# A decoder layer on one TensorE: the pooling mixer's value projection as two Strassen units inside the gates' pass

## The chip, the cores and the metric

The kernel runs on one core of a Trainium2 chip. The metric is the device time of one execution in microseconds. The table further down gives three runs and one profiled execution.

## The reference, cut to what matters

One layer is computed on 1040 rows: 16 learned meta tokens, then 1024 tokens of width 1024. All data are float32. The part that the change touches:

```python
u = rmsnorm(h, mix_norm_pre[l])
proj = u @ w_in[l]
q, f_logit, i_in, g_out, v_pool, gate_a, gate_b = jnp.split(proj, cuts, axis=-1)
a = hgrn2(q, f_logit, i_in, g_out, lbs[l], hgrn_out_norm[l])
p = multiscale_pool(v_pool, pool_proj[l], pool_scale[l])
z = (sigmoid(gate_a) * (a @ w_branch_hgrn[l]) + sigmoid(gate_b) * (p @ w_branch_pool[l]))
```

`q`, `f_logit`, `i_in`, `g_out` and `v_pool` are 512 wide, the two gates 1024. `hgrn2` is a gated recurrence over four heads of 128, evaluated in chunks; the gate `g_out` multiplies its output at the end. `multiscale_pool` takes for each of four groups of 128 channels the mean over the last 2, 4, 8 or 16 rows less the row itself, and then a 128x128 matrix for each group. After `z` come `w_out`, a norm, a gated feed-forward part with a causal convolution (width 2816) and another norm.

## The kernel before, in words

Every float32 product is made of three matmuls: each operand is split into a rounded high part and the rest, and high times high, high times low and low times high are added in PSUM. Features lie in partitions and rows (time) in the free dimension. `uhi` and `ulo` hold the normed input as eight blocks of 128 features by 1040 rows. SBUF work space is a pool of 24 equal slots of 1040 floats (`slot`, line 89); a tile that is taken when all are in use waits for a release. Weights go through rings of three buffers each (`wraw`, `whi`, `wlo`).

The stages in order:

1. The value pass (up to line 1057) norms the input, transposes it and computes `i_in` for the heads. While it ends, sums of quarters of the input are begun (`gate_steps`, line 966), for Strassen. `SUMS_AT` (line 39) says after which step which part of these sums is put in the queues.
2. Two early output gates (`EARLY_G` = 2), G0 and G1, are plain projections (`proj`, line 175: 8 feature blocks, 3 chunks of rows, 3 passes, 72 matmuls). Their sigmoids go to DRAM (`gscr`, line 777) and are read back when their head needs them (line 752).
3. The gates' pass (lines 997 to 1083). Class `Strassen` (line 191) computes 256 columns at a time, a unit, with seven products in place of eight, of half the features and about half the rows each. P1, P2, P6 and P4 stream 514 columns (two halo rows more), P3, P5 and P7 512. A product of 514 is cut in two (line 276). Eight units make both gates. The first `EARLY` = 4 units, in pairs, have P1 and P2 computed ahead (`start_pair`, line 322), because these two need no sums; the result of P1 is kept in a slot. The other products come in `rest` (line 328). `load_unit` (line 240) loads a unit's weights and has POOL add four sums of them; `ahead` (line 211) splits the operands of the next four products, on ACT and DVE (for some of the early ones on POOL, line 230). `put_gate` (line 838) adds up the results on DVE, takes the sigmoid on ACT and stores to DRAM.
4. The head pass (lines 1103 to 1133), in the order written in `ORDER` (line 45): F, Q, G and PV are projections of 72 matmuls, `c` is the chain of gate arithmetic with cumulative sums (`chain_f`, line 592), `h` the next of eight steps of a head (`head_steps`, line 612), PP the 128x128 matrix of a pooling group, `sp` the mean and split ahead of it (`pool_split`, line 808), `sa` the split of a head's output, BB and BA the branch products, and `w` the splitting of weights for the feed-forward part. PV (`post_pv`, line 792) copies the projection to `vp` and has POOL make the trailing sums by doubling. `eng` and `POOLED` (line 48) say which elementwise steps go to POOL instead of DVE. In a head's steps 2 to 4 matmuls make decayed scores for six levels, which masked copies put into `sc` (`level_out`, line 657: eight copies of 64 columns, one for each chunk; line 725: one of 128 columns for each chunk). Step 6 builds the chunk states (`ds`, `st`), step 7 the output (`po`), step 8 norms it (`ms`).
5. `w_out`, the feed-forward part and the last norm, which also use Strassen.

In the value pass and in the early part of the gates' pass the order on ACT, DVE and PE is the program's (line 1002). Elsewhere a planner orders the instructions of each engine by its own costs and by the order in which they are written. Each engine's queue is strictly in order; nearly all transfers are issued on SP's queue, also in order. Transfers that add into DRAM, in the feed-forward part, are issued on POOL (lines 1308, 1309, 1326).

Of the kernel before, what the change touches and what calls it, by code (L numbers as in the profile page):

```python
# [14 lines left out]
P = 128  # L15
D = 1024
SEQ = 1024
NM = 16
# [29 lines left out]
POOLED = ("e1k.0 e1k.3 kdmul.2 kdmul.3 kdsub.2 lk32.1 lk4.1 lk64.0 lq16.1 lq16.3 lq32.0 lq32.1 lq32.2 lq4.0 "  # L48
          "lq64.0 lq64.3 lq8.0 lq8.1 lq8.2 osg.2 qsmul.2 qsmul.3 sub2.2 sub32.1 sub4.1 sub8.1 sub8.3 wBA2 wBA6 "
          "wBA7 wBB2 wF0 wF2 wF3 wPP2 wPV0 wPV1 wPV2 wPV3 wQ0 wQ1 wQ3").split()  # L50
# [7 lines left out]
def trunk_kernel(ctx: ExitStack, tc: tile.TileContext, x, meta_tokens, mix_norm_pre,  # L58
# [10 lines left out]
    sm = ctx.enter_context(tc.tile_pool(name="sm", bufs=4))  # L69
# [19 lines left out]
    def slot(n, dtype=F32, name="s"):  # L89
        return stage["fm", "p"].tile([P, n], dtype, tag="fm", name=nm(name), padded_shape=[P, L])  # L90

    def ubig(dtype, name, n=KD * L):
        return upool.tile([P, n], dtype, tag="u", name=nm(name), padded_shape=[P, KD * L])
# [19 lines left out]

    open_pool("fm", FM_SLOTS)
    open_pool("ps", 8, PSUM)
# [75 lines left out]
    class Strassen:  # L191
# [8 lines left out]
        def __init__(self, units, run, early, quarters, halo, put, whole):  # L200
            self.units, self.run, self.early, self.bq = units, run, early, quarters
            self.halo, self.put, self.whole = halo, put, whole
# [65 lines left out]
        def product(self, u, p, onto=None):  # L268
# [19 lines left out]
            self.ahead(self.lead)  # L288
            return x if onto is not None else (x if self.whole_pair else x[:, o0 : o0 + n])
# [3 lines left out]
        def span(self, u, p="P1"):  # L293
# [3 lines left out]
            return (0, 512 - HN // 2 - HALO, HT) if self.halo(u) else (HALO, 0, HN)  # L297

        def own(self, u, t):
            return t[:, HALO:] if self.halo(u) else t  # L300

        def half(self, key, i, n, name):

            if key not in self.halves:
                self.halves[key] = slot(2 * HT, name=name)
            return self.halves[key][:, i * HT : i * HT + n]
# [107 lines left out]
    uhi = uhi_f.rearrange("p (k t) -> p k t", k=KD)  # L414
    ulo = ulo_f.rearrange("p (k t) -> p k t", k=KD)
# [148 lines left out]

    def V(c, h):
# [7 lines left out]

# [18 lines left out]
    def chain_f(h, kk, b, f, f2):  # L592
# [8 lines left out]
        for t0, rows in row_tiles:  # L601
            dve.tensor_tensor_scan(b[:, t0 : t0 + rows], f[:, t0 : t0 + rows], f[:, t0 : t0 + rows],
                                   0.0, ALU.add, ALU.bypass)
# [8 lines left out]
    def head_steps(h):  # L612
# [44 lines left out]
        def level_out(lv, ps, pm):  # L657
            if lv >= 32:
# [5 lines left out]
                return  # L664
            o4 = sc.rearrange("p (c b two h) -> p c b two h", c=NCH, two=2, h=lv)[:, :, :, 1, :]
            p4 = ps.rearrange("p (c b h) -> p c b h", c=NCH, h=lv)
            m3 = masks[lv].rearrange("p (b h) -> p b h", h=lv)
            for c in range(NCH):
                dve.copy_predicated(o4[:, c], m3, p4[:, c])
# [48 lines left out]
        for j in range(2):  # L718
# [4 lines left out]
            for i in range(4):  # L723
                c = 4 * j + i
                dve.copy_predicated(sc[:, c * P : (c + 1) * P], mbase, ps[:, i * P : (i + 1) * P])
# [24 lines left out]
        if h < EARLY_G:  # L750
            sgs[h] = slot(TQ, name="sg")
            nc.sync.dma_start(sgs[h], sgd[h])
# [20 lines left out]
        sg = sgs[h]  # L773
        eng(f"osg.{h}").tensor_tensor(o, o, sg, ALU.mult)
        heads[h] = dict(o=o)

    sgd = dram.tile([EARLY_G, P, TQ], F32, name="gscr")

    def post_g(h, pg):
        sg = slot(TQ, name="sg")  # L780
        for (lo, n), ps in zip(CH_Q, pg):
            act.activation(sg[:, lo : lo + n], ps[:, :n], AF.Sigmoid)
        if h < EARLY_G:
            nc.sync.dma_start(sgd[h], sg)
        else:
            sgs[h] = sg


    pooled, pin = {}, {}
    phi, plo = [None] * HEADS, [None] * HEADS  # L790

    def post_pv(g, pv):
        w = POOL_WINDOWS[g]
        vp, s1 = slot(L, name="vp"), slot(L, name="s1")
        s2 = slot(L, name="s2") if w > 2 else None
        for (lo, n), ps in zip(CH_ALL, pv):
            act.copy(vp[:, lo : lo + n], ps[:, :n])
# [8 lines left out]
        pooled[g] = (cur, vp)  # L806

    def pool_split(g):
        w = POOL_WINDOWS[g]
        cur, vp = pooled[g]  # L810
# [6 lines left out]
        pin[g] = split(cur[:, T0:L], "pl")  # L817
# [18 lines left out]
    sd = dram.tile([2 * KD, P, TQ], F32, name="sscr")  # L836

    def put_gate(u, i, h, a, b, c=None):
        at = slice(HT, TQ) if h else slice(0, HT)
# [5 lines left out]
        nc.sync.dma_start(sd[2 * u + i, :, at], g)  # L845

# [18 lines left out]
    def job(kind, i):  # L865
# [6 lines left out]
        if kind == "PV":  # L872
            return (wblock(WIN, 0, KD, CV + i * P, P), KD, u_all, CH_ALL, lambda r: post_pv(i, r))
# [72 lines left out]
    for q, i, t0, n in (("b11", 0, T0, HT), ("b21", 1, T0, HT), ("b22", 1, T0 + HT, HN)):  # L946
# [3 lines left out]
    def two_halves(dst, q):  # L950
        n = HN if q in ("t1", "t3") else HT
# [3 lines left out]
    def halo_sums(bq, d):  # L955
# [4 lines left out]
        t4 = small([P, 4 * HALO], "t4", "t4", 2).rearrange("p (k t) -> p k t", k=4)  # L960
# [5 lines left out]
    def gate_steps(d):  # L966
# [4 lines left out]
        s_ = slice(d.start - HALO, d.stop - HALO)  # L971
        a, b = (slice(T0 + d.start + o, T0 + d.stop + o) for o in (0, 512))
# [4 lines left out]
        else:  # L977
# [18 lines left out]
    ds = [slice(0, HALO)] + [slice(HALO + i * P, HALO + (i + 1) * P) for i in range(4)]  # L996
    gates = Strassen([(WIN, c + 2 * P * j) for c in (CA, CB) for j in range(KD // 2)], range(KD), EARLY, gq,
                     lambda u: True, put_gate, lambda u, i: None)
# [3 lines left out]
    with tc.manual_schedule(engines={E.Activation, E.DVE, E.PE}):  # L1002
# [34 lines left out]
        for i in range(2, len(vtiles)):  # L1037
# [11 lines left out]
            if i == 5:  # L1049
                for q in ("t2", "t1", "t3", "t4"):  # L1050
                    two_halves(gq, q)
                sums = [gate_steps(d) for d in ds]
            if i == len(vtiles) - 1:
                gl = Loader([job("G", h)[:2] + (P,) for h in range(EARLY_G)])
# [3 lines left out]
        gates.load_first(0)  # L1058
        gates.load_first(1)
        gates.ahead(2)  # L1060
        for h in range(EARLY_G):
            src, n_k, xs, chunks, post = job("G", h)
            r = proj(None, 0, n_k, xs, chunks, ws=gl.next(), name="pg")
            for j in SUMS_AT.get(9 + 2 * h, ()):
                next(sums[j], None)
            post(r)
            if h == 0:
                dve.tensor_tensor(vmeta[:NM], vm_hl[:NM], vm_low[:NM], ALU.add)
                gates.load_first(2)
                gates.ahead(4)  # L1070
            for j in SUMS_AT.get(10 + 2 * h, ()):
                next(sums[j], None)
# [3 lines left out]
        gates.load_first(3)  # L1076
# [603 lines left out]
```

## Time and profile before

| what | us |
|---|---|
| median of three runs | 1365.33 |
| lowest and highest of them | 1363.51, 1367.08 |
| the profiled execution | 1363.17 |
| its span, first to last instruction | 1361.5 |
| PE busy | 1336.0 |
| DVE busy | 952.4 |

PE is TensorE's matmuls, PEld its weight loads, DVE VectorE, ACT ScalarE, POOL GpSimd, SP SyncE. Matmuls overlap: one has a duration, but the next may start before it ends, so what matmuls cost is read from the distance of their starts. A group's row has its line, engine, operation, tiles and shapes, count, busy time, mean duration of one in ns, and the idle time of the engine before them with what ended it. A row "A <- B" tells that engine and tile A waited for B.

### The profile page before, as it was taken

Reading aid. Unit: us, or ns where it says so; the run is one execution under the profiler, and the core shown is the slowest. Engines: PE = TensorE matmul, PEld = TensorE weight load, DVE = VectorE, ACT = ScalarE, POOL = GpSimd, SP = SyncE. Lnnn points to the kernel's source line nnn. Section 1 sums busy time; section 2 is a strip of 40 time slices with the busy share of each in tenths; the row PEclk is TensorE's granted clock in tenths of the full one; section 3 lists DMA queues with packets and bytes.
Section 4 is the critical chain, followed back from the end, with each engine's and each line's share of the span. In section 5 each row is a group of like instructions: output and inputs, shape, how many; then the busy total and the mean of one; then the engine's idle time right before and its main releaser. Section 6 shows DMA issues by size and latency. Waiting matters only on the chain. (4 is left out here: it accounts for less than half of the span.)

```text
span 1361.5 us, 20285 instructions
## 1 busy us (share of the span) xinstructions
PE 1336.0 (98%) x7737; PEld 1181.8 (87%) x7737; DVE 952.4 (70%) x1414; ACT 565.9 (42%) x946; POOL 439.2 (32%) x326
## 2 busy tenths in 40 slices
PE   8999999999999999999999999999999999999997
PEld 7799899999999899987778888888888887888786
DVE  6754644388886768665568888888878776744557
ACT  6543333367455474225654222222222223543343
POOL 2015421237444600051021655454566742000100
PEclk9999999999999999999999999999999999999999
DMA  7134333311110158999876877756677799965624
GB/s 266 44 115 146 117 116 108 101 54 41 34 49 19 34 173 278 323 283 310 289 259 238 225 204 201 201 173 169 158 180 157 173 243 273 386 207 186 186 62 170
DMA packets 141455, 236.68 MB, mean 174 GB/s; under 512 B 9254, under 2 KB 77450, under 8 KB 141358
## 3 DMA queue, kind: packets, MB, share of 16 engines
q1 hardware_dynamic: 129294, 211.00, 46.2%
q0 software_dynamic: 12064, 24.38, 10.6%
q8 instruction: 61, 1.00, 0.3%
q14 instruction: 36, 0.29, 0.1%
HBM read 171.85 MB, written 86.53 MB: 190 GB/s over the span
## 5 line engine op out<-in xcount | busy, mean ns | idle before, releaser
L284 PE MATMUL P<-v,whi 128*128 128x512 f32 (+2 forms) x408 | 141.5, 354 | 2.1 <-ACT p L1486 1.2
L285 PE MATMUL P<-v,whi 128*128 128x512 f32 (+2 forms) x408 | 141.0, 353 | 0.0
L287 PE MATMUL P<-v,wlo 128*128 128x512 f32 (+2 forms) x424 | 135.6, 350 | 0.0
L172 PE MATMUL pd<-rot 128*128 128x512 f32 x272 | 106.0, 390 | 0.3 <-DVE rot L1413 0.3
L173 PE MATMUL pd<-rot 128*128 128x512 f32 x272 | 106.0, 390 | 0.0
L138 POOL TENSOR_TENSOR wlo<-wraw,whi 128x1024 fp32r<-128x1024 f32 (+1 forms) x19 | 45.8, 2415 | 164.6 <-ACT whi L137 94.8
L1413 DVE TENSOR_TENSOR rot<-yt,rot 128x1024 fp32r<-128x1024 f32 x33 | 41.2, 1250 | 71.6 <-ACT rot L1412 71.6
L284 PEld LDWEIGHTS P<-v,whi 128*128 128x128 f32 x408 | 76.8, 188 | 13.1 <-ACT p L1486 1.4
L229 ACT CAST whi<-wraw 128x512 fp32r<-128x512 f32 x78 | 46.1, 618 | 97.7 <-PE P L285 86.9
L285 PEld LDWEIGHTS P<-v,whi 128*128 128x128 f32 x408 | 76.9, 189 | 10.6
L287 PEld LDWEIGHTS P<-v,wlo 128*128 128x128 f32 x424 | 74.2, 188 | 11.0
L1301 POOL TENSOR_TENSOR ys<-y 128x512 f32<-128x512 f32 x22 | 35.3, 1603 | 139.6 <-issue 95.9
L230 DVE TENSOR_TENSOR wlo<-wraw,whi 128x512 fp32r<-128x512 f32 x74 | 65.4, 905 | 19.9 <-ACT whi L229 19.9
L171 PE MATMUL pd<-rot 128*128 128x512 f32 x272 | 72.8, 391 | 2.1 <-ACT rot L1412 1.2
L255 POOL TENSOR_TENSOR swa<-wraw,wraw 128x512 f32<-128x512 f32 x28 | 44.5, 1589 | 90.7 <-DMA wraw<-in_w_in_dram 60.7
L1412 ACT CAST rot<-yt 128x1024 fp32r<-128x1024 f32 x33 | 34.6, 1051 | 90.1 <-PE pd L172 90.1
L229 ACT CAST whi<-swa 128x512 fp32r<-128x512 f32 x56 | 33.4, 618 | 88.0 <-PE P L285 79.3
L137 ACT CAST whi<-wraw 128x1024 fp32r<-128x1024 f32 (+1 forms) x28 | 26.4, 943 | 100.3 <-PE ppv L185 19.6
L1345 DVE SCALAR_TENSOR_TENSOR y<-g,par,y 128x1024 f32<-128x1024 f32 x44 | 64.3, 1462 | 0.8
L171 PEld LDWEIGHTS pd<-rot 128*128 128x128 f32 x272 | 50.9, 188 | 13.7 <-ACT rot L1412 2.0
L229 ACT CAST whi<-swb 128x512 fp32r<-128x512 f32 x56 | 33.4, 619 | 67.2 <-PE P L285 63.1
L172 PEld LDWEIGHTS pd<-rot 128*128 128x128 f32 x272 | 51.1, 188 | 11.3 <-DVE rot L1413 0.7
(387 smaller groups left out, 4187.2 us busy)
## 6 DMA issues: line engine op xcount, KB each, us to landing
wraw<-in_w_in_dram SPq DMA_DIRECT2D x36, 512.0 KB
yt<-ysum SPq DMA_DIRECT2D x33, 512.0 KB
wraw<-in_ffn_w_gate_dram SPq DMA_DIRECT2D x26, 512.0 KB
wraw<-in_w_out_dram SPq DMA_DIRECT2D x24, 512.0 KB
wraw<-in_ffn_w_up_dram SPq DMA_DIRECT2D x22, 512.0 KB
wsum<-in_ffn_w_down_dram SPq DMA_DIRECT2D x22, 512.0 KB
ysum<-ys SPq DMA_DIRECT2D x11, 768.0 KB
sa<-sscr SPq DMA_DIRECT2D x16, 513.0 KB
```

The costliest lines, as they stand in the source:

```text
L138: eng.tensor_tensor(lo, raw, rr(hi), ALU.subtract)
L171: pe.matmul(ps, ahi, bhi, start=first, stop=False)
L172: pe.matmul(ps, ahi, blo, start=False, stop=False)
L173: pe.matmul(ps, alo, bhi, start=False, stop=last)
L229: act.copy(hi, src)
L230: (pool_e if 4 <= i < 2 * self.early else dve).tensor_tensor(lo, src, rr(hi), ALU.subtract)
L255: pool_e.tensor_tensor(s1, a21, a22, ALU.add)
L284: pe.matmul(d, whi[:, k, :], xh[:, c : c + w], start=(k == 0 and onto is None), stop=False, **go)
L285: pe.matmul(d, whi[:, k, :], xl[:, c : c + w], start=False, stop=False, **go)
L287: pe.matmul(x[:, o : o + w], wlo[:, k, :], xh[:, c : c + w], start=False, stop=(k == 3), **go)
L1345: dve.scalar_tensor_tensor(a, g[:, j : j + SEQ], cvw[:, j, m : m + 1], a, ALU.mult, ALU.add)
L1413: dve.tensor_tensor(lo, src, rr(hi), ALU.subtract)
```

## The change

- The four PV projections and their job kind go. `v_pool` is computed by two more Strassen units in the gates' pass, numbered 8 and 9 (`V_UNIT`), run fourth and seventh (`GATE_RUN`). They need all 1040 rows, so the quarters of the input now start at row 0, with all 16 meta rows in the first ones: quarters of 528 and 512 rows (`HF`, `HN`), and P1, P2, P6 and P4 of a V unit stream 528 columns, cut in 264 and 264. Gate units still stream 514.
- POOL's trailing sums, the mean and the split are a generator (`pool_sums`); one step of it is put in the queues after each product. The split rows are stored to DRAM (`pscr`) and read back (`load_pooled`, `l` in `ORDER`) ahead of PP.
- All eight gate units, not four, have P1 and P2 computed ahead (`EARLY_G` is now that number). The gates' pass begins right after the value pass, and `SUMS_AT` puts the remaining sums of quarters behind the early products.
- G0 and G1 are computed in the head pass like G2 and G3, with no store and reload; `ORDER` is rewritten.
- The masked copies of a level are one instruction for eight chunks, those of line 725 one for four. The cumulative sum of `chain_f` is one scan of 1040 with a row of ones and zeros that restarts it at each chunk, in place of nine scans.
- Slots are 1088 floats (4352 bytes) and 26 of them; the large tiles have the same row length. The scratch for POOL's transfer descriptors is set to 2048 bytes. One scratch tile of the last stage moves into a slot.

```diff
-EARLY_G = 2
-SUMS_AT = {5: (2,), 6: (2, 1), 8: (3,), 9: (1, 3), 10: (1, 4), 11: (4, 0), 12: (0, 0)}
-FM_SLOTS = 24
+HF = HN + NM
+EARLY_G = 8
+SUMS_AT = {5: (2,), 6: (2, 1), 8: (3,), 9: (1, 3), 10: (1,), 11: (4,), 12: (4,), 13: (0,), 14: (0,), 15: (0,)}
+FM_SLOTS = 26
+LP = 1088
+GS = 0
+V_UNIT = KD + GS // 2
+GATE_RUN = [0, 1, 2, V_UNIT, 3, 4, V_UNIT + 1, 5, 6, 7]
...
-ORDER = ("F0 c0 Q0 h0 F1 h0 c1 Q1 h0 h1 F2 h1 c2 h0 Q2 h1 h2 G2 h0 h1 h2 h0 F3 h0 h2 c3 PV0 h1 h2 h1 Q3 h3 h1 h3 h1 "
-         "PV1 h3 sp0 PV2 h2 h3 sa1 sp1 sp2 PP0 h2 PV3 h2 h3 sp3 PP1 h0 G3 w0 h3 PP2 h3 PP3 w1 BB0 w4 h2 BB1 w4 BB2 "
-         "w4 sa2 BB3 w5 h3 BB4 w5 BB5 w5 sa0 sa3 BA0 w5 BA1 w2 BB6 w3 BA2 BB7 BA3 BA4 BA5 BA6 BA7")
+ORDER = ("F0 c0 Q0 h0 F1 h0 c1 Q1 h0 h1 F2 h1 c2 h0 Q2 h1 h2 G0 h0 h1 h2 h0 F3 h0 c3 h2 h1 G1 h2 h1 Q3 h1 h3 G2 l0 "
+         "h3 h1 h2 PP0 l1 h3 G3 h2 h3 sa1 PP1 l2 h2 h3 l3 PP2 h0 w0 h3 PP3 w1 BB0 w4 h2 BB1 w4 h3 BB2 w4 sa2 BB3 "
+         "w5 h3 BB4 w5 BB5 w5 sa0 sa3 BA0 w5 BA1 w2 BB6 w3 BA2 BB7 BA3 BA4 BA5 BA6 BA7")
...
             self.ahead(self.lead)
+            if self.tasks:
+                next(self.tasks[0], None) or self.tasks.pop(0)
...
-            return (0, 512 - HN // 2 - HALO, HT) if self.halo(u) else (HALO, 0, HN)
+            e = self.extra(u)
+            return self.most - e, (HN - e) // 4 * 2 if e else 0, HN + e
...
-        for t0, rows in row_tiles:
-            dve.tensor_tensor_scan(b[:, t0 : t0 + rows], f[:, t0 : t0 + rows], f[:, t0 : t0 + rows],
-                                   0.0, ALU.add, ALU.bypass)
+        dve.tensor_tensor_scan(b, keep_on, f, 0.0, ALU.mult, ALU.add)
...
-            m3 = masks[lv].rearrange("p (b h) -> p b h", h=lv)
-            for c in range(NCH):
-                dve.copy_predicated(o4[:, c], m3, p4[:, c])
+            m4 = masks[lv].rearrange("p (o b h) -> p o b h", o=1, h=lv).to_broadcast([P, NCH, nb, lv])
+            dve.copy_predicated(o4, m4, p4)
...
-            for i in range(4):
-                c = 4 * j + i
-                dve.copy_predicated(sc[:, c * P : (c + 1) * P], mbase, ps[:, i * P : (i + 1) * P])
+            dve.copy_predicated(sc[:, j * 512 : (j + 1) * 512].rearrange("p (c t) -> p c t", c=4),
+                                mbase.rearrange("p (o t) -> p o t", o=1).to_broadcast([P, 4, P]),
+                                ps.rearrange("p (c t) -> p c t", c=4))
...
+    def pool_sums(g, vp):
...
             pool_e.tensor_tensor(nxt[:, a:L], cur[:, a:L], cur[:, a - step : L - step], ALU.add)
             cur, step = nxt, 2 * step
+            yield True
...
         dve.scalar_tensor_tensor(cur[:, T0:L], cur[:, T0:L], 1.0 / w, vp[:, T0:L], ALU.mult, ALU.subtract)
-        pin[g] = split(cur[:, T0:L], "pl")
+        yield True
+        for i, t in enumerate(split(cur[:, T0:L], "pl")):
+            nc.sync.dma_start(pd[g, i], rr(t))
+
+    def load_pooled(g):
+        pin[g] = [slot(TQ, F32R, "pl") for _ in range(2)]
+        for i, t in enumerate(pin[g]):
+            nc.sync.dma_start(rr(t), pd[g, i])
...
     def put_gate(u, i, h, a, b, c=None):
+        if u >= V_UNIT:
+            if (u, i) not in vps:
+                vps[u, i] = slot(L, name="vp")
+            d = vps[u, i][:, slice(HF, L) if h else slice(0, HF)]
+            dve.tensor_tensor(d, a, b, ALU.add)
+            if c is not None:
+                dve.tensor_tensor(d, d, c, ALU.add)
+            return
...
+    def whole_gate(u, i):
+        if u >= V_UNIT:
+            gates.tasks.append(pool_sums(2 * (u - V_UNIT) + i, vps.pop((u, i))))
...
+    gate_units = [(WIN, c + 2 * P * j) for c, n in ((CA, KD), (CB, KD), (CG, GS), (CV, HEADS)) for j in range(n // 2)]
+    gates = Strassen(gate_units, GATE_RUN, EARLY_G, gq,
+                     lambda u: NM if u >= V_UNIT else HALO, put_gate, whole_gate, NM)
...
-        for e in range(0, EARLY, 2):
+        at = len(vtiles)
+        for e in range(0, EARLY_G, 2):
+            for i in (e + 3, e + 4):
+                if i < EARLY_G:
+                    gates.load_first(i)
             p = gates.start_pair(e)
             for f in [f[i] for i in range(2) for f in p]:
                 f()
-                for j in SUMS_AT.get(13, ()) if e == 0 else ():
+                for j in SUMS_AT.get(at, ()):
                     next(sums[j], None)
+                at += 1
...
-    nc = _bacc.Bacc("TRN2", target_bir_lowering=False, num_devices=1)
+    nc = _bacc.Bacc("TRN2", target_bir_lowering=False, num_devices=1, dynamic_dma_scratch_size=2048)
```

More of the change, by code (lines that the diff above doesn't have):

```diff
@@ L413, in trunk_kernel @@
     uhi_f, ulo_f = ubig(F32R, "uhi"), ubig(F32R, "ulo")
-    uhi = uhi_f.rearrange("p (k t) -> p k t", k=KD)
-    ulo = ulo_f.rearrange("p (k t) -> p k t", k=KD)
+    uhi, ulo = (u.rearrange("p (k t) -> p k t", k=KD)[:, :, U0:] for u in (uhi_f, ulo_f))
     WIN = w_in[0]
@@ L1050, in trunk_kernel @@
                 for q in ("t2", "t1", "t3", "t4"):
-                    two_halves(gq, q)
+                    two_halves(gq, q, HF)
                 sums = [gate_steps(d) for d in ds]
+            if i == len(vtiles) - 2:
+                gates.load_first(0)
+                gates.load_first(1)
             if i == len(vtiles) - 1:
-                gl = Loader([job("G", h)[:2] + (P,) for h in range(EARLY_G)])
+                gates.ahead(4)
+                gates.load_first(2)
             for j in SUMS_AT.get(i, ()):
@@ L1057, in trunk_kernel @@
             v_out(ps, vtiles[i][0])
[L1058 to L1072, printed above, removed]
+        dve.tensor_tensor(vmeta[:NM], vm_hl[:NM], vm_low[:NM], ALU.add)
         close_pool("ps")
         open_pool("pf", 4, PSUM)
-        gates.load_first(3)
-        for e in range(0, EARLY, 2):
+        at = len(vtiles)
[3 more added lines that the diff above has]
+                    gates.load_first(i)
             p = gates.start_pair(e)
@@ L1080, in trunk_kernel @@
                 f()
-                for j in SUMS_AT.get(13, ()) if e == 0 else ():
+                for j in SUMS_AT.get(at, ()):
                     next(sums[j], None)
+                at += 1
     gates.finish()
+    for task in gates.tasks:
+        for _ in task:
+            pass
     close_pool("pf")
```

95 lines of the change are left out of this document (44 added, 51 removed).

## The prediction

> **What bounds the kernel now.** I read the page first, then who PE waited for in the part that the diff touches, then a table of stages, then starts of single matmuls, because a busy PE here can hide a slow one.
>
> ```profile
> span 1361.5 us, 20285 instructions
> PE 1336.0 (98%) x7737; PEld 1181.8 (87%) x7737; DVE 952.4 (70%) x1414; ACT 565.9 (42%) x946; POOL 439.2 (32%) x326
> ```
>
> TensorE is busy for 98% of the span and no other engine comes near. The program's time falls only if TensorE gets less to do, or loses a wait. The waits of PE from 60 to 594 us (engine, line, what released it: us in total, times, longest) are all of these:
>
> ```profile
> PE ppv L184 <- ACT st L735: 2.5, 1, 2.5
> PE pbb L184 <- ACT whi L147: 1.0, 1, 1.0
> PE sb L722 <- POOL kk L705: 0.6, 1, 0.6
> PE pf L184 <- DVE sc L663: 0.5, 1, 0.5
> PE P L284 <- ACT sg L782: 0.2, 1, 0.2
> PE sl L649 <- DVE d L634: 0.2, 1, 0.2
> ```
>
> They sum to 5.0 us, so in these 534 us there is little idle time to win and a good deal to lose. The stages, cut where PE changes jobs (stretch: length, busy us and instructions of PE, PEld, DVE, ACT, POOL, clock, DMA share, GB/s):
>
> ```profile
> 67.00:90.40 23.40, 23.18 (x147) 22.81 (x145) 20.05 (x47) 12.77 (x38) 0.00 (x0) 1.00 0.44 124
> 90.40:248.80 158.40, 158.38 (x1056) 145.76 (x1057) 74.60 (x103) 55.16 (x95) 55.44 (x38) 1.00 0.37 118
> 248.80:370.80 122.00, 120.69 (x894) 118.75 (x892) 99.66 (x203) 67.27 (x102) 53.59 (x24) 1.00 0.19 56
> 370.80:408.30 37.50, 37.50 (x304) 36.80 (x303) 28.12 (x64) 21.31 (x35) 17.32 (x10) 1.00 0.15 45
> 408.30:489.20 80.90, 78.43 (x576) 75.40 (x575) 54.20 (x104) 42.06 (x72) 38.30 (x18) 1.00 0.10 29
> ```
>
> The first row is the two early output gates with the gates' quarter sums beside them, the second the eight Strassen units of the gates, the other three the head pass, the last of them from the end of Q3 to the `ds` step of head 3. PE is full in all; DVE is next with 82% in the third row and 67% in the fifth. Clock 1.00 throughout: no throttle to reckon with here.
>
> The durations of matmuls overlap, so cost is the distance of starts (start, duration, engine, line):
>
> ```profile
> 159.90 0.40 PE L284 MATMUL P<-t1h,whi 128*128 128x512 f32 x1
> 160.13 0.40 PE L285 MATMUL P<-t1l,whi 128*128 128x512 f32 x1
> ...
> 90.42 0.39 PE L284 MATMUL P<-uhi,whi 128*128 128x258 f32 x1 [0.24 <-ACT sg L782]
> 90.64 0.29 PE L285 MATMUL P<-ulo,whi 128*128 128x258 f32 x1
> 90.77 0.28 PE L284 MATMUL P<-uhi,whi 128*128 128x256 f32 x1
> ...
> 248.82 0.33 PE L184 MATMUL pf<-uhi,whi 128*128 128x348 f32 x1
> ...
> 335.14 0.40 PE L184 MATMUL pg<-uhi,whi 128*128 128x342 f32 x1
> 346.55 0.38 PE L712 MATMUL pt<-ident,kd 128*128 128x128 f32 x2
> ...
> 378.55 0.41 PE L184 MATMUL ppv<-uhi,whi 128*128 128x348 f32 x1
> ...
> 390.08 0.49 PE L712 MATMUL pt<-ident,kd 128*128 128x128 f32 x3
> ```
>
> 512 columns start every 0.23 us, 258 every 0.13: 0.45 ns a column. One PV job runs from 378.55 to 390.08, 11.53 us for 72 matmuls; one G job from 335.14 to 346.55, 11.41 us. The eight gate units run from 90.42 to 248.82: 158.40/8 = 19.80 us a unit.
>
> **The change, part by part.** *PV becomes two Strassen units.* Removed from PE: 4 x 11.53 = 46.1 us. Added: two units. A unit of the gates has four products of 514 columns, each in cuts of 258 and 256 (4 k-tiles x 3 passes x 2 = 24 matmuls), and three of 512. A V unit needs all 16 meta columns and not two, so its four products have 528 columns in two cuts of 264: 96 matmuls with 7 columns more on average, 7 x 0.45 = 3.1 ns, 0.3 us. So 20.1 us a unit, 40.2 us for both. **PE: 40.2 - 46.1 = -5.9 us.** In columns: 4 x 24 x 1040 = 99,840 against 2 x 12 x (4 x 528 + 3 x 512) = 87,552, and 12,288 x 0.45 ns = 5.5 us: the same within the rounding.
>
> *Output gates all late.* G0 and G1 move from 67 us to the head pass: 2 x 11.41 us leave one place and come to the other, 0 on PE. Their two stores and two reloads of 513 KB on SP go. Their cover goes too: 20.05 us of DVE beside them, mostly quarter sums. Now 16 products P1 and P2 of all eight gate units come first, 16 x 24 x about 0.12 = 46 us, before P6 needs the first sum; SUMS_AT puts the remaining sums behind the first seven. That is more cover than before, so I cost it at nothing. If it failed, P2's results would leave PSUM late: four pairs of banks give three products, 8.6 us, of slack. Four more units split their weights early: four more loads of 512 KB on SP, and 8 more subtractions on POOL.
>
> *Pool's sums, means and splits move into the gates' pass.* The rows of the head pass (line, engine, shape, count | busy us, mean ns), POOL's for the stretch from 370 us:
>
> ```profile
> L816 DVE SCALAR_TENSOR_TENSOR s<-s,vp 128x1026 f32<-128x1026 f32 x4 | 8.2, 2055 | 0.1
> L822 DVE TENSOR_TENSOR pll<-s,plh 128x1026 fp32r<-128x1026 f32 x4 | 6.0, 1495 | 0.0
> ...
> L804 POOL TENSOR_TENSOR s<-s 128x1037 f32<-128x1037 f32 (+2 forms) x6 | 13.8, 2308 | 1.8 <-issue 1.4
> L804 POOL TENSOR_TENSOR s<-vp 128x1039 f32<-128x1039 f32 x4 | 7.7, 1921 | 4.5 <-ACT vp L797 4.5
> ```
>
> DVE: 14.2 us leave the head pass; POOL: 21.5 us. In the gates' pass they come on top of two units of casts and results (a quarter of 74.60, 55.16 and 55.44 us) and, on DVE, at most the 20 us of the first row: DVE 74.6 + 18.7 + 14.2 + 20 = 128, POOL 55.4 + 13.9 + 21.5 + the 8 subtractions, about 100, of 158.4 + 40.2 = 198.6 us. Covered by PE. One step is taken after each product, so a POOL sum waits for DVE's `vp`; behind it on POOL stand the weight sums of the next unit, which the casts of P6 need. With half of POOL free I cost that at nothing. SP gets 8 stores and 8 loads of 513 KB, 8.4 MB, at DMA shares of 0.37 and 0.10 to 0.19: hidden. SBUF: in the first rest I count 16 quarter tiles, 4 kept P1 pairs, 4 weight sums and 2 results on their way out, 26 of 26 slots; before, two pairs fewer and 24. Tight as before, no new wait assumed.
>
> *Merged copies and the scan.*
>
> ```profile
> L669 DVE COPY_PREDICATED sc<-mask,sl 128x64 f32<-128x64 uint8 x128 | 19.6, 250 | 9.6 <-PE sl L649 9.5
> L725 DVE COPY_PREDICATED sc<-mbase,sb 128x128 f32<-128x128 uint8 x32 | 7.0, 297 | 9.9 <-PE sb L722 9.9
> L602 DVE TENSOR_TENSOR_SCAN b<-f 128x128 f32<-128x128 f32 x32 | 12.6, 469 | 0.0
> ```
>
> 64 elements take 0.153 us of DVE (19.6/128), 128 take 0.219: 1.03 ns an element, so 512 in one go 0.62 us. Bounds: 0.22 (length free) and 8 x 0.153 = 1.22 (nothing saved). I take 0.62, on the line of both rows: 16 x 0.62 = 9.9 for 19.6, and 8 x 0.62 = 5.0 for 7.0. The scan over 1040 elements lies between one piece, 0.39, and eight, 3.2 (12.6/4); I take 2.4, nearer the eight: -3. DVE's head pass falls by 14.2 + 9.7 + 2.0 + 3 = 29 us; the weights of two more G jobs put some 4 us back. All of it lies beside PE, worth nothing by itself.
>
> *What the head pass loses as cover.* PE there: -46.1 + 22.8 = -23.3 us. DVE: 182.0 - 25 = 157 of 217, 72%, against 76% of 240.4. No engine becomes the bound. The largest wait, 2.5 us before PV3, has its cause in what moves. Two rows of the tiles `st` and `pll` (who waited: us, times):
>
> ```profile
> DVE pll L822: 3.2, 1
> ...
> ACT st L735: 3.2, 1
> ```
>
> ACT's copy of `st` stood behind DVE's split of the pooled rows, and PV3 behind that: -2.5 us. What is late next is head 3. From Q3's end to its `ds` step PE had 80.9 us of work and waits; now 80.9 - 2.5 - 3 x 11.5 + 11.4 = 55.3. DVE there: 54.2 - 13 - 3 + 2 = 40, 73% against 67%. Two steps of head 3 now have only small jobs ahead of them. A new wait there lies between 0 and about 10 us: DVE idled 26.7 us in that stretch, and were all of it forced, 40 + 26.7 - 55.3 = 11. The nearest rows are the six waits above, 0.2 to 2.5; I take 2.0 in all.
>
> *4352-byte rows, 26 slots, smaller DMA scratch:* no instruction more or less; 0.
>
> **Sum:** -5.9 - 2.5 + 2.0 = **-6.4 us**. The profiled execution took 1363.17 us (span 1361.5 and 1.7 around it) and would take 1356.8. It lies 2.16 us under the median of the runs, so for the median 1365.33 - 6.4 = **1358.9 us**.
>
> **Where a page speaks against it.** The Trainium skill, "TensorE: Matmul & The Clock Gate", section "Back-to-back issue gap", gives a sustained stream 81 ns a matmul at 128 columns and 131 ns at 512. By that estimate a column costs 0.13 ns and PE would save only about 3 us. The trace disagrees, with 0.23 us at 512.
>
> **The rivals.** *The waits eat it.* The head pass loses 23 us of cover, and each of head 3's steps, or the first branch product with its weights, waits 1 to 3 us. For it: 67 to 73% DVE in the last stretch, and only 5.0 us of waits now, which can hardly shrink. Against: DVE's own work there falls. With 4 to 10 us of new waits: 1361 to 1367, say 1363.
>
> *Pooled rows come late (slower).* Place: SP, in order, ahead of PP2 and PP3. Their rows are now loads, asked for one short job ahead, in a queue that waits for weight buffers (longest wait last):
>
> ```profile
> SPq L134 <- POOL wlo L138: 124.8, 12, 23.6
> ...
> SPq L146 <- DVE wlo L138: 15.0, 1, 15.0
> ```
>
> One such wait of 15.0 us with nothing over it gives -6.4 + 15.0 = +8.6, 1374. It decides once it reaches 6.4 us (no change) and 10.5 us (slower by 0.3%). Against: the rows lie in DRAM long before, and POOL's weight splits that made the 23.6 us are mostly PV's, which go.
>
> *Spacing doesn't follow columns.* If a matmul cost the same at 264 as at 347, 0.16 us by the PV job, 264 matmuls for 288 would save 3.8 us and the waits decide: 1361.5. The rows of 256 to 512 columns speak against it.
>
> *The scratch throttles POOL's transfers.* If each of the feed-forward part's accumulating transfers had to land before the next is issued, POOL would be late there; no row bounds it better than zero to the stage's free POOL time:
>
> ```profile
> 718.00:1141.00 423.00, 420.89 (x2293) 363.74 (x2291) 349.74 (x437) 127.09 (x213) 218.79 (x165) 1.00 0.74 196
> ```
>
> POOL has 204 us free, so even 3 us for each of the 66 issues (11 x 4 and 11 x 2 in the code) stay covered; 0.3 us more on each would add 20 us, 1379.
>
> **How the numbers follow.** Forecast (1353 to 1361) 0.60; waits eat it 0.25; pooled rows late 0.10; spacing 0.03; scratch 0.02. A measurement here tells 0.3%, 4.1 us, from no change. Faster by that: 0.60. Within: 0.25 + 0.03 = 0.28. Slower: 0.10 + 0.02 = 0.12. The range: the low end is every wait gone, -5.9 - 5.0 = -10.9, and the 1.8 us by which runs lie around their median: 1353. The high end takes in the second case: 1367.5. It leaves out the late rows and the scratch, 0.12, and a little below.
>
> **What would show it.** The gates' pass with ten units should last about 198 us with PE full; the head pass should lose 23 us; no wait of PE for ACT `st` behind `pll`. A wait of `pp` jobs for a DMA, of `pt`, `sb` or `sl` for POOL or DVE over 2 us, or of a product P for DVE in the gates' pass would prove me wrong, as would a V unit over 21 us.

## The result, and the profile after

The changed kernel takes 1366.83 us (median of 20 runs, 1362.82 to 1369.99) against 1365.36 us for the kernel before in the same session (20 runs). The ratio is 1.0007, 95% interval [0.9999, 1.0014]: no change that can be measured, where 6.4 us less was forecast. The time is 7.9 us above the forecast 1358.9, inside its range and in the part of it that belongs to the case "the waits eat it". The profiled execution took 1369.69 us, one of the slower ones.

Its page begins (span; then busy us, share of the span and instructions):

```profile
span 1368.0 us, 20130 instructions
PE 1335.3 (98%) x7713; PEld 1179.4 (86%) x7713; DVE 973.2 (71%) x1266; ACT 576.3 (42%) x954; POOL 444.1 (32%) x340
```

PE has 24 matmuls fewer, but is busy for only 0.7 us less, in a span 6.5 us longer: PE also counts as busy in the stretches at half clock, shown further down, and they hide most of the saving. These are the waits of PE from 60 to 610 us in the changed kernel (line, what released it: us, times, longest):

```profile
PE P L292 <- DVE sg L855: 1.8, 1, 1.8
PE pbb L191 <- ACT whi L154: 1.6, 1, 1.6
PE sb L730 <- DVE plo L833: 1.3, 1, 1.3
PE pq L191 <- ACT sg L787: 1.3, 1, 1.3
PE P L292 <- DVE sg L853: 1.2, 1, 1.2
PE po L770 <- DVE st L752: 1.0, 1, 1.0
PE sl L657 <- DVE d L642: 0.9, 1, 0.9
PE pbb L195 <- DVE wlo L155: 0.9, 1, 0.9
PE sl L657 <- issue: 0.7, 1, 0.7
PE P L292 <- ACT v L515: 0.7, 1, 0.7
PE sb L730 <- DVE sc L677: 0.6, 1, 0.6
PE po L769 <- DVE sc L671: 0.4, 1, 0.4
PE ppp L192 <- DMA pl<-pscr: 0.4, 1, 0.4
```

They sum to 12.8 us, against 5.0 before. The wait of 2.5 us for ACT `st` is gone as forecast, but thirteen small ones stand in place of six, and two of them (L853, L855) are waits of a product P for DVE in the gates' pass, one of the signs that were named as proof against the forecast.

The gates' pass and the rest up to `w_out` in the changed kernel (stretch: length, busy us of PE, PEld, DVE, ACT, POOL, clock, DMA share, GB/s):

```profile
67.59:269.15 201.56, 198.39 (x1321) 183.71 (x1322) 133.61 (x174) 74.93 (x141) 104.11 (x66) 0.99 0.47 138
269.15:602.08 332.93, 323.82 (x2282) 313.94 (x2281) 238.59 (x313) 176.46 (x267) 75.41 (x43) 0.98 0.41 135
```

The same two stretches in the kernel before, the first with its two early output gates in it:

```profile
67.00:248.82 181.82, 181.58 (x1203) 168.59 (x1202) 94.65 (x150) 67.92 (x132) 55.44 (x38) 1.00 0.38 119
248.82:593.63 344.81, 340.01 (x2426) 332.24 (x2425) 256.78 (x489) 174.44 (x271) 118.64 (x57) 1.00 0.36 118
```

The gates' pass lasts 201.6 us where about 198 were forecast, and the second stretch lost 11.9 us where the head pass was to lose 23. DVE and POOL have in the gates' pass nearly what the forecast gave them (133.6 and 104.1 us for 128 and about 100), 66% and 52% of the time. The averages were right and the conclusion, that PE covers them, was not. The clock column is new: 0.99 and 0.98 where the rows of before had 1.00. It is low in short stretches of 3.41 us. Here are two such places, each behind the stretch ahead of it:

```profile
237.50:240.96 3.46, 1.62 (x14) 1.44 (x13) 3.42 (x6) 1.14 (x2) 2.19 (x3) 1.00 0.17 63
240.96:244.37 3.41, 3.41 (x18) 3.41 (x17) 1.35 (x3) 1.23 (x2) 3.41 (x3) 0.50 0.56 164
...
561.50:565.23 3.73, 1.89 (x11) 1.31 (x9) 0.68 (x1) 2.16 (x3) 0.00 (x0) 1.00 1.09 373
565.23:572.05 6.82, 6.22 (x22) 6.22 (x23) 5.35 (x9) 2.05 (x3) 0.00 (x0) 0.50 1.01 343
```

In each pair PE is busy for about half of the first stretch, because it waits, and then runs at a granted clock of 0.50 in the next, though by then it has work. Each 3.41 us at half clock do 1.7 us less work. Up to 602 us the changed kernel's profile has four such stretches (one at 241.0, one at 377.5, two from 565.2), the one of before none: 6.8 us.

Why DVE is late at 237 us is in its timeline and POOL's in the changed kernel (start, duration, line, operation, tiles):

```profile
228.96 2.31 DVE L813 SCALAR_TENSOR_TENSOR s<-s,vp 128x1026 f32<-128x1026 f32 x1
231.19 1.78 DVE L238 TENSOR_TENSOR wlo<-swa,whi 128x512 fp32r<-128x512 f32 x1
232.90 2.94 DVE L826 TENSOR_TENSOR pll<-s,plh 128x1026 fp32r<-128x1026 f32 x1
235.76 0.67 DVE L853 TENSOR_TENSOR sg<-p,P 128x512 f32<-128x512 f32 x1
236.35 2.69 DVE L238 TENSOR_TENSOR wlo<-swb,whi 128x512 fp32r<-128x512 f32 x2
238.97 0.67 DVE L855 TENSOR_TENSOR sg<-sg,P 128x512 f32<-128x512 f32 x1
```

```profile
230.26 2.16 POOL L266 TENSOR_TENSOR swb<-wraw,swa 128x512 f32<-128x512 f32 x1
232.38 2.37 POOL L805 TENSOR_TENSOR s<-vp 128x1039 f32<-128x1039 f32 x1
235.98 1.92 POOL L805 TENSOR_TENSOR s<-s 128x1037 f32<-128x1037 f32 x1 [1.23 <-DVE pll L826]
```

DVE has no gap. The mean (L813), the weight split and the pooled rows' low part (L826) stand in its queue ahead of `sg` at L853 and L855, which take results out of PSUM, and PE waits 1.8 us for a bank. The subtractions are also slow beside POOL. A group of the changed kernel gives the comparison (count, busy us, mean ns, idle): the same subtraction, same shape, for the pooled rows here and for head outputs later.

```profile
L826 DVE TENSOR_TENSOR pll<-s,plh 128x1026 fp32r<-128x1026 f32 x4 | 8.8, 2200 | 0.0
...
L826 DVE TENSOR_TENSOR al<-o,ah 128x1026 fp32r<-128x1026 f32 x4 | 5.7, 1434 | 0.0
```

2.20 us beside 1.43. The Trainium skill, "SBUF — State Buffer", section "Who interferes with whom", says that a DVE instruction with two SBUF inputs contends with a GpSimd instruction that reads SBUF, and that the order of issue decides which of them is held back. The trace agrees: the subtraction of 2.94 us begins at 232.90 beside a sum of POOL that runs to 234.75, while L853, with one input in PSUM, keeps its 0.67 us beside POOL's next sum. (That POOL begins that one only at 235.98 says nothing on this: its row has it waiting for `pll`.)

### The profile page after: what moved, and what is told of

It is laid out like the page before. It is cut to its first block, busy times and chain, and to the rows that moved or that the text cites. A ratio compares the mean times of both kernels' runs of the same rounds, so it can differ in the third digit from the quotient of the medians.

```text
span 1368.0 us, 20130 instructions
## 1 busy us (share of the span) xinstructions
PE 1335.3 (98%) x7713; PEld 1179.4 (86%) x7713; DVE 973.2 (71%) x1266; ACT 576.3 (42%) x954; POOL 444.1 (32%) x340
## 5 line engine op out<-in xcount | busy, mean ns | idle before, releaser
L237 ACT CAST whi<-wraw 128x512 fp32r<-128x512 f32 x84 | 49.8, 617 | 93.5 <-PE P L293 75.8
L292 PEld LDWEIGHTS P<-v,whi 128*128 128x128 f32 x408 | 77.2, 189 | 12.8 <-DVE p L354 1.3
L145 POOL TENSOR_TENSOR wlo<-wraw,whi 128x1024 fp32r<-128x1024 f32 (+1 forms) x15 | 34.3, 2287 | 135.2 <-DMA wraw<-in_w_out_dram 74.5
L263 POOL TENSOR_TENSOR swa<-wraw,wraw 128x512 f32<-128x512 f32 x30 | 47.7, 1591 | 68.3 <-DMA wraw<-in_ffn_w_gate_dram 21.8
L144 ACT CAST whi<-wraw 128x1024 fp32r<-128x1024 f32 (+1 forms) x24 | 22.2, 925 | 100.4 <-PE pf L192 32.9
L292 PE MATMUL P<-t2h,whi 128*128 128x258 f32 (+2 forms) x212 | 61.7, 308 | 1.8 <-DVE sg L855 1.8
L238 DVE TENSOR_TENSOR wlo<-swa,whi 128x512 fp32r<-128x512 f32 x60 | 56.9, 958 | 8.5 <-ACT whi L237 8.4
```

Source lines behind the costliest of these rows:

```text
L237: act.copy(hi, src)
L238: (pool_e if 4 <= i < 2 * self.early else dve).tensor_tensor(lo, src, rr(hi), ALU.subtract)
L263: pool_e.tensor_tensor(s1, a21, a22, ALU.add)
L292: pe.matmul(d, whi[:, k, :], xh[:, c : c + w], start=(k == 0 and onto is None), stop=False, **go)
```

## The experiments

Ratios are to the kernel before. The time that half clock takes is worked out for a kernel as span times (1 - granted clock), a mean over its executions: 5.8 us for the changed kernel, 4.3 for the one before (35 executions of another session; the standard errors are 0.5 and 0.3). Not all of it need be lost, since some can fall where PE would wait anyway: by a straight line through the 20 executions of the changed kernel, a us of it made the time 0.74 us longer.

**DVE's queue in the gates' pass: a1_sums, a2_poolsplit, d1_both.** The first spreads the quarter sums over more early products, the second gives the subtraction to POOL, the third does both.

```diff
-SUMS_AT = {5: (2,), 6: (2, 1), 8: (3,), 9: (1, 3), 10: (1,), 11: (4,), 12: (4,), 13: (0,), 14: (0,), 15: (0,)}
+SUMS_AT = {5: (2,), 6: (2, 1), 8: (3,), 9: (1,), 11: (3,), 12: (1,), 14: (4,), 16: (4,), 18: (0,)}
```

```diff
-        for i, t in enumerate(split(cur[:, T0:L], "pl")):
+        hi, lo_ = slot(TQ, F32R, "plh"), slot(TQ, F32R, "pll")
+        act.copy(hi, cur[:, T0:L])
+        pool_e.tensor_tensor(lo_, cur[:, T0:L], rr(hi), ALU.subtract)
+        for i, t in enumerate((hi, lo_)):
```

> The changed kernel with SUMS_AT spread out: the remaining sums of quarters are queued after products 0, 2, 3, 5, 7 and 9 of the gates' pass, not after 0 to 3. Theory W (new waits of PE, from DVE and POOL work that was moved in front of results PE needs): the wait of 1.4 us near 87 us, a product P for DVE's first sigmoid sums, goes; the time falls by 1.4 us, or 3.1 us where a stretch at half clock followed it. Theory C (the time is set by how many 3.4-us stretches at half clock fall into a run): the time hardly moves, under 0.5 us, since that wait was followed by none in the trace. Rival D (DVE's load in the head pass is what counts): 0.

> The changed kernel with the low part of the pooled rows subtracted on POOL and not on DVE. Theory W: in the changed kernel DVE took 2.94 us for one of these subtractions beside POOL, ahead of a gate's result, and PE waited 2.0 us near 238 us with a half-clock stretch after it. The wait goes: -2.0 us, with the stretch -3.7 us. Rival: POOL's subtraction, about 2.4 us each, delays POOL's sums of the next unit's weights and a wait of the same size comes there: 0.

> The changed kernel with both repairs of the gates' pass: the sums spread out and the low part of the pooled rows on POOL. Theory W: both of its waits (1.4 and 2.0 us) and the half-clock stretch behind the second go, -3.4 us at full clock, -4 to -5 us of the mean: 0.3% faster than before. Theory C: the stretches come elsewhere, -1 us.

Measured: a1_sums 1366.57, ratio 1.0001 [0.999, 1.0013]; a2_poolsplit 1365.16, 0.9995 [0.9984, 1.0007]; d1_both 1364.22, 0.9986 [0.9973, 0.9998]. Each edit takes away its own wait (1.2 us for L853, 1.8 us for L855); with both, PE waits nowhere in the gates' pass behind its first matmul, and it lasts 196.05 us for 201.56. (That first matmul waits 0.7 us for `v` in every version that has the change.) One edit alone can't be told from the changed kernel; the two together give 2.6 us of median, where 4 to 5 had been expected: half clock still takes 5.9 us of an execution. DVE's queue was one cause, but it is not the whole.

**Cover in the head pass: f1_order, g1_orderonly.** Cover is the work that PE has while another engine finishes a step. f1_order is d1_both with each of the later output gates one block later in ORDER; g1_orderonly is the changed kernel with this alone.

```diff
-... F3 h0 c3 h2 h1 G1 h2 h1 Q3 h1 h3 G2 l0 h3 h1 h2 PP0 l1 h3 G3 h2 h3 sa1 PP1 l2 h2 h3 l3 PP2 ...
+... F3 h0 c3 h2 h1 Q3 h2 h1 h3 G1 h1 l0 h3 h1 h2 PP0 l1 h3 G2 h2 h3 sa1 PP1 l2 G3 h2 h3 l3 PP2 ...
```

> Both repairs of the gates' pass, and in ORDER every late output gate one large block later: Q3 takes the place of G1, G1 that of G2, G2 that of G3, and G3 stands between head 3's fourth and fifth step, where PE had only small jobs. Theory W with short cover as the cause: the waits for DVE between head 3's fifth step and PP2 (1.0, 1.3 and 0.4 us) and Q3's wait for the sigmoids of G1 (1.3 us) go, -3 to -4 us against the kernel with both repairs. Rival (DVE's total is the limit, waits only move): 0.

> The changed kernel with the later output gates of f1_order alone: the sums of quarters and the split of the pooled rows stay as the change has them, so the two waits of the gates' pass (1.8 and 1.2 us) stay. In f1_order against d1_both the head pass lost about 4 us of waits. If these were cover alone (output gates put where head 3's steps need them), the same 4 us go here: about 1362.5 us, 0.998 of the kernel before, gates' pass 201.5 us, head pass about 223. Rival: the order pays only because the gates' pass ends with DVE free, since DVE and ACT carry a backlog into the head pass: then about 1366 us, head pass 227 us.

Measured: f1_order 1360.21 us, 0.995 [0.9934, 0.9966]; g1_orderonly 1362.03, 0.9982 [0.997, 0.9993]. Against the changed kernel's median that is 4.8 us less for the order alone, 2.6 for DVE's part alone, 6.6 for both: they nearly add up, so the order doesn't need the freed DVE. By the ratios, each to the kernel before in its own session, it is 3.4, 2.9 and 7.8 us, each uncertain by about 2, so the times alone don't say which of the two parts is larger. The waits of PE in f1_order from 60 to 610 us are all of these:

```profile
PE pbb L191 <- ACT whi L154: 1.5, 1, 1.5
PE sl L657 <- issue: 1.0, 1, 1.0
PE sl L657 <- DVE d L642: 0.9, 1, 0.9
PE pm L178 <- DVE sa L872: 0.8, 1, 0.8
PE pbb L195 <- DVE wlo L155: 0.8, 1, 0.8
PE P L292 <- ACT v L515: 0.7, 1, 0.7
PE pbb L192 <- DVE plo L836: 0.5, 1, 0.5
```

6.2 us in seven waits. Those for `st`, `sc`, `scm` and `pscr` are gone, and so is that of `pq` for ACT's `sg`. This version beats both kernels, with the change's work on PE untouched, and lies 1.3 us above the forecast.

**The merged copies: a3_unmerged, a4_merged.** The changed kernel with copies and scan in pieces again, and the kernel before with them merged.

```diff
-            m4 = masks[lv].rearrange("p (o b h) -> p o b h", o=1, h=lv).to_broadcast([P, NCH, nb, lv])
-            dve.copy_predicated(o4, m4, p4)
+            m3 = masks[lv].rearrange("p (b h) -> p b h", h=lv)
+            for c in range(NCH):
+                dve.copy_predicated(o4[:, c], m3, p4[:, c])
```

(and likewise the copies of the base level and the scan; a4_merged is the reverse)

> The changed kernel with the masked copies and the scan in pieces, as before the change. Rival D (DVE's load in the head pass sets its waits): DVE's head pass grows by some 10 to 15 us and PE's waits there by at least 3 us: +3 to +6 us. Theory W with short cover as the cause (chains of a head, not DVE's total): under 1.5 us either way.

> The kernel before with the merged masked copies and the one scan alone. My prediction priced them at nothing, since all of it lies beside PE: 0, within 1 us. Rival D: the waits of the head pass before (5 us in all) shrink: -1 to -4 us.

Measured: a3_unmerged 1369.14, 1.0038 [1.0022, 1.0054]; a4_merged 1367.16, 1.001 [0.9999, 1.0021]. In pieces, the changed kernel waits 2.7 us for the copies where it waited 0.6:

```profile
PE sb L733 <- DVE sc L680: 2.7, 1, 2.7
```

Before the change, with four PV jobs as cover, merging brings nothing; with less cover it keeps 2.3 us of median from being lost, in part through the clock (half clock takes 8.1 us of an execution in a3_unmerged for 5.8). DVE time gained is worth something only where DVE ends last.

**More and less moved: b1_half, b2_gs4.** b1_half takes groups 2 and 3 of the value projection as one unit and leaves groups 0 and 1 as projections in the head pass; b2_gs4 (GS = 4) takes the output gates too as Strassen units.

```diff
-GATE_RUN = [0, 1, 2, V_UNIT, 3, 4, V_UNIT + 1, 5, 6, 7]
+GATE_RUN = [0, 1, 2, 3, V_UNIT + 1, 4, 5, 6, 7]
...
+        if kind == "PV":
+            return (wblock(WIN, 0, KD, CV + i * P, P), KD, u_all, CH_ALL, lambda r: post_pv(i, r))
```

```diff
-GS = 0
+GS = 4
```

> Half of the change: one V unit, for pooling groups 2 and 3, in the gates' pass; groups 0 and 1 are projections PV1 and PV0 in the head pass again, PV0 in the thin stretch ahead of head 3's last steps, and group 2 and 3's PP come first. PE's work against before falls by half, 2.95 us. Theory W with short cover as the cause: against the whole change PE gets 2.95 us more work, and of the seven waits from 415 to 500 us (about 7 us) at least half go: within 1 us of the changed kernel or faster. Rival (DVE's total, not cover, sets them): the same waits stay, +2 to +3 us.

> Twice the dose: the four output gates become two more Strassen units of the gates' pass (GS = 4), so PE has another 4 x 11.41 - 2 x 19.8 = 6.0 us less to do, and the head pass another 45.6 us less cover. Theory W: DVE's head pass (about 160 us of work and its idle time) no longer fits under some 172 us of PE; new waits of 10 us and more, +4 to +20 us over the changed kernel, and more half-clock stretches. If cover does not matter: -6 us.

Measured: b1_half 1374.81, 1.0061 [1.0045, 1.0077]; b2_gs4 1409.1, 1.0317 [1.0295, 1.0339]. From the waits of b1_half:

```profile
PE ppp L191 <- DMA pl<-pscr: 2.8, 1, 2.8
...
PE ppp L191 <- ACT st L743: 1.5, 1, 1.5
```

and of b2_gs4:

```profile
PE sl L653 <- DVE d L642: 12.0, 3, 5.7
PE sl L657 <- DVE d L642: 10.6, 3, 6.2
PE sl L653 <- POOL d L641: 8.7, 1, 8.7
```

In b1_half the pooled rows come late through DRAM, the third case of the forecast; the sums of two groups are formed in the head pass there, not long ahead of their use. In the changed kernel that wait is 0.4 us. So b1_half, 8 us slower than the changed kernel where no more than 1 had been expected, is no clean half of the change. b2_gs4 saves more work on PE and is 44 us slower than before and 42 slower than the changed kernel, where 4 to 20 had been expected: without output gates between them the head steps wait for their own elementwise work, and half clock takes 39.7 us of an execution for 4.2. It shows the price of cover, waits and clock together.

**Slots and scratch: c1_slots.** The kernel before with 26 slots of 1088 and the small scratch.

```diff
-FM_SLOTS = 24
+FM_SLOTS = 26
...
-    nc = _bacc.Bacc("TRN2", target_bir_lowering=False, num_devices=1)
+    nc = _bacc.Bacc("TRN2", target_bir_lowering=False, num_devices=1, dynamic_dma_scratch_size=2048)
```

> The kernel before with 26 slots of 1088 floats, the scratch of 2048 bytes and the scratch tile in a slot, and nothing else. My prediction priced that at 0: within 1 us. Rival (the smaller scratch holds POOL's accumulating transfers up, in the feed-forward part): that part's PE waits grow by 2 us or more.

Measured: 1369.07, 1.0019 [1.0005, 1.0033]. From start to start of their first matmuls, the feed-forward part's first half lasts 437.13 us for 436.58, so the scratch costs next to nothing there. The loss, where less than 1 us had been expected, goes with the clock: half clock takes 6.7 us of an execution for 4.2 in the kernel before, 2.5 us more where the means differ by 2.7, and in the profiled execution three stretches of it fall in the head pass, where the kernel before has none. PE's waits from 60 to 610 us are no reason: they sum to 5.2 us for 5.0. Why new slots shift the clock isn't settled.

**Waits and the clock: e1_few, e2_many.** The kernel before with waits put into the gates' pass: a small matmul that ACT holds back, 6 long ones or 24 short ones.

```diff
+            late = self.late.get((u, p), 0)
+            if late:
+                t16 = small([P, 16], "late", "late", 2)
+                for _ in range(late):
+                    act.copy(t16, self.prev[:, 256:272])
+                pe.matmul(x[:16, o0 : o0 + 16], t16, t16, start=True, stop=True)
...
+    gates.late = {(u, "P3"): 9 for u in range(1, 7)}
```

(e2_many: `{(u, p): 1 for u in range(8) for p in ("P5", "P3", "P7")}`)

> The kernel before with six waits of PE put in by hand in the gates' pass, one before P3 of units 1 to 6: a small matmul on a tile that ACT writes nine times in a row after the product before, about 2 us each, 12 us in all. Theory C (an idle stretch of about 2 us makes the clock fall to half for the next 3.4 us, which costs another 1.7 us): 12 us plus three to six such stretches, +17 to +22 us over before. If the clock does not follow idle time: +12 us.

> The same amount of idle time in small pieces: 24 waits of about 0.5 us, before P5, P3 and P7 of all eight units, 12 us in all. Theory C: no piece is long enough in a window of 3.4 us, no more half-clock stretches than before: +12 us, 5 us or more less than with six long waits. Rival (the clock falls with the idle share of any stretch): as many as with the six.

Measured: e1_few 1387.17, 1.0148 [1.0116, 1.0181]; e2_many 1404.52, 1.0269 [1.0236, 1.0302]. The waits that were put in, first in e1_few, then in e2_many:

```profile
PE P L281 <- ACT late L280: 13.8, 6, 2.7
```

```profile
PE P L281 <- ACT late L280: 26.3, 24, 1.7
```

The short waits came out twice as long as meant, 1.1 us on average, so the pair doesn't compare equal sums, and e2_many, expected at least 5 us below e1_few, lies 17 us above it. Half clock takes 11.8 us of an execution in e1_few, 7.0 in e2_many, 5.4 in the kernel before beside them. So 13.8 us in six long waits bring 6.4 us of half clock, and 26.3 us in 24 short ones 1.6, hardly clear of the noise (the standard errors of 7.0 and 5.4 are 0.6 and 0.8). In the profile of e1_few four of the six are followed by a stretch of half clock, in that of e2_many one of 24. The times differ far less: 21.8 us over the kernel before for 13.8 us of waits, and 39.1 for 26.3, which is 1.6 and 1.5 us for each us of wait. In the profiles the gates' pass is 22.0 and 37.5 us longer; past the waits and the half clock 1.4 and 9.5 us remain, 0.2 and 0.4 us for each interruption, which the rows of waits don't count. The first place with half clock in e1_few:

```profile
149.00:152.05 3.05, 0.53 (x3) 0.09 (x1) 1.29 (x2) 2.46 (x11) 0.00 (x0) 1.00 0.59 207
152.05:155.46 3.41, 3.23 (x9) 2.61 (x10) 0.69 (x1) 0.12 (x1) 2.78 (x3) 0.50 0.00 0
```

## Why the prediction was wrong, point by point

**PE's work** (forecast -5.9 us): right, a little better. In the gates' pass of f1_order, free of waits, 192 matmuls of 264 columns start every 0.1215 us and 72 of the V units' 512 every 0.2268: 23.3 + 16.3 = 39.7 us for both units, 40.2 forecast. The pass lasts 196.05 us, 198 forecast. (258 columns start every 0.120 us on average in the kernel before, not 0.13 as the single rows suggest; a column is then 0.44 ns for 0.45.)

**"That is more cover than before, so I cost it at nothing"** and **"With half of POOL free I cost that at nothing"**: failed. DVE at 66% and POOL at 52% of the pass do have room on average, but the value groups' sums and subtractions come in a burst, in strict order ahead of the additions that empty PSUM, and stretched by each other. The slack of three products named there did not hold. Price: 1.2 + 1.8 us of waits; taking both away (d1_both) was worth 2.6 us of median. In the trace half clock follows the longer one, but its mean over the executions did not fall with them.

**"I take 2.0 in all"** for new waits in the head pass: failed, and by the waits of the trace this is the larger term. From the head pass on, the changed kernel's waits sum to 9.1 us, where they were 4.8 before, though the 2.5 us ahead of PV3 went: 6.8 us new. They are what the case "the waits eat it" describes, and a better order alone (g1_orderonly) won 4.8 us of median back. The step behind the failure: cover was counted over the whole stretch from Q3 to `ds`, 55.3 us of PE against 40 of DVE. What counts is what PE has between one step of a head and the next, and two output gates stood where it had enough. In f1_order six of these waits, 5.0 us, are gone, for two small new ones of 1.3; those of the branch product `pbb` for its split weights, 2.5 us, are not steps of a head and stay at 2.3.

**"No throttle to reckon with here"**: failed. The clock was read from one profile whose rows had none. By the mean granted clock the changed kernel has 1.5 us more of half clock for each execution, worth 1.1 us at the 0.74 above. The trace shows half clock behind two places with new waits, but where the extra 1.5 us come from stays open: it does not clearly go when those waits go (d1_both has 5.9 us beside 4.2 in the kernel before of its session, f1_order 6.0 beside 5.4), and c1_slots has 6.7 beside 4.2 with the new slots and hardly more waits.

**"4352-byte rows, 26 slots, smaller DMA scratch: ... 0"**: not borne out in the kernel before, where c1_slots costs 0.7 to 4.5 us (ratio 1.0005 to 1.0033). Whether the changed kernel pays as much was not tried; what it pays through the clock is in the 1.1 us.

**Together**: 5.9 us saved and 2.7 us of old waits gone; against them 3.0 us in the gates' pass, 0.7 ahead of it, 6.8 in the head pass and 1.1 of clock, 11.6. That gives +3.0, where the medians give +1.5; the terms are from one profiled execution and no better than a us or so (with PE's saving as measured, 6.4 and the 1.4 of the last section, it is +1.1). The time lies inside the range, and the case that came true, "the waits eat it", had been given 0.25.

**Right**: the wait for `st`; the scratch at nothing for the feed-forward part; the pooled rows not late on SP (0.4 us). The merged copies took longer than taken: of the changed kernel's groups,

```profile
L677 DVE COPY_PREDICATED sc<-mask,sl 128x512 f32<-128x512 uint8 x16 | 13.7, 853 | 0.4 <-PE sl L657 0.3
```

0.85 us for 0.62 forecast, inside the bounds of 0.22 and 1.22; the scan took 2.32 for 2.4. "Worth nothing by itself" holds in the kernel before (a4_merged); in the changed one it is worth 0.3% (a3_unmerged against it).

Open: why c1_slots and the changed kernel have more half clock; and whether the output gates have a still better order, which was tried for one order only.

## What to carry to other kernels

When TensorE is full, work taken from it is worth its time only if each step of a dependent chain keeps enough other matmuls between it and the next: count cover step by step, not over a stage, and when a job that served as cover goes, move the jobs that are left. A second engine's share of busy time doesn't say that it is on time; look at what stands in its queue ahead of the instructions that free PSUM. And count what an interruption costs beyond the wait that is listed: six long waits brought half clock, twenty-four short ones 0.4 us each that no row shows, and in time a us of wait cost about 1.5 us either way.

## What the runs showed of the hardware that was not expected

**The clock answers to single waits.** In fourteen profiles, from 70 to 1330 us, every stretch of half clock (f1_order has none) lasts 3.41 us or a multiple, on a grid that is fixed within an execution and falls differently in the next. Laid on that grid, a stretch at full clock in which matmuls covered at most 0.46 of the time was followed by half clock 29 times of 29; between 0.47 and 0.62 it was 4 of 26; above that it happened 8 times, each where the matmuls stream few columns, 59 to 72 on average, and cover 0.72 to 1.00 of the stretch. Many stretches like these were not followed by half clock, so few columns alone don't explain it. The one at 377.5 us in the changed kernel is of this kind. The stretch ahead of it, and the stretch itself:

```profile
374.08:377.49 3.41, 3.41 (x30) 3.10 (x29) 3.37 (x8) 3.41 (x7) 0.14 (x1) 1.00 0.08 22
377.49:380.91 3.42, 3.42 (x17) 3.42 (x17) 3.42 (x4) 1.50 (x4) 1.15 (x1) 0.50 0.00 0
```

The Trainium skill, "TensorE: Matmul & The Clock Gate", section "What's actually happening", describes such a free-running window of 3413 ns, and the trace agrees. Section "Why this matters for your kernels" of the same page warns of gaps over about 3 us; here waits of 1.8 to 2.9 us sufficed where they fell into one stretch of the grid.

**One collision of 1 us decides a later wait.** The same two instructions in the changed kernel (first fence) and in g1_orderonly (second), with the same program up to there:

```profile
78.99 1.84 DVE L381 TENSOR_TENSOR t3l<-tt,t3h 128x256 fp32r<-128x256 f32 x2
```

```profile
78.97 0.75 DVE L381 TENSOR_TENSOR t3l<-tt,t3h 128x256 fp32r<-128x256 f32 x2
```

POOL's weight subtraction beside it, at 79.07 and 79.05, took 1.48 us in the first and 2.50 in the second: one of the two is held back by the other. In the first DVE stays 1.1 us behind, and PE's wait of 1.2 us for L853 follows; in the second there is none. So a part of that 1.2 us isn't a1_sums' own: it also goes by chance.

**512-column matmuls got 2% shorter** in the gates' pass, in the kernel before and then in f1_order:

```profile
L284 PE MATMUL P<-t1h,whi 128*128 128x512 f32 x32 | 12.7, 396 | 0.0
```

```profile
L292 PE MATMUL P<-t1h,whi 128*128 128x512 f32 x40 | 15.6, 390 | 0.0
```

Their starts are 227 ns apart for 232, about 1.4 us over the 288 of the gate units. c1_slots still has 231, so it isn't the rows of 4352 bytes; the new cut of the quarters remains as a possible reason, and wasn't tried by itself.
